# Hybrid decoder layer: turning q for two attention units at once, and moving the tokens' scales of the first part into the second

## The chip, the core and the metric

The kernel is written for one Trainium2 core and runs on one. Five engines work from their own queues, in the order of each queue, and wait for each other by semaphores: TensorE (PE, matmuls and transposes), VectorE (DVE), ScalarE (ACT), GpSimd (POOL) and SyncE (SP, which here only issues DMAs). The metric is the device time of one execution in microseconds (us); less is better.

## What is computed

One layer of a decoder with attention and a short convolution side by side, in float32: 512 tokens, width 2048.

```python
h = rms_norm(x, norm_gain)
q, k, v, g_attn, c_b, c_c, c_h, g_conv = split(h @ w_in)
q, k = partial_rope(rms_norm(q, q_gain)), partial_rope(rms_norm(k, k_gain))   # 16 and 4 heads of 64
y_attn = sliding_window_attention(q, k, v, sinks) * silu(g_attn)              # window 128
y_conv = c_b * conv3(c_c * c_h) * silu(g_conv)
x = x + concat(y_attn, y_conv) @ w_out
gate = sigmoid(rms_norm(x, gate_gain) @ w_ple_gate + b_ple_gate)
x = x + gate * rms_norm(p @ w_ple_proj, ple_gain)
```

The attention's probabilities are `exp(s - m) / (sum + exp(sink - m))` with `s` the scaled scores inside the window.

## The kernel before

Every float32 product is made of three: operands are split into a rounded high half and a low rest (`halves`: an ACT cast, then a DVE subtraction), and PE multiplies high by high, low by high and high by low. The large matmuls save products by a fast scheme of blocks (`run_step`, line 241), which needs sums of weight blocks (L189) and their halves (L199, L200) in time for each step. One step is 12 matmuls of 128x512.

The program has three parts. The **first** makes k and v (L515) and then q in 28 steps (L241). `kv` are four tiles of 128x512 in the pool `rowp`, one for each block of 128 tokens; q is left in four quarters `qs[t, n]`, `t` a half of the tokens and `n` a half of the heads. x enters unnormalised, so the tokens' scale `r_x = rsqrt(mean x^2)` is applied later: `tok["x"]` is that scale and `rx2_tok` its square. For the norm of q's heads `square_q` sums squares into `rq[t, n]` (called `msq`), and `rstd_q` makes of it the factor: DVE multiplies by `rx2_tok` (L566) and scales (L301), POOL takes the power -1/2 (L306), and DVE multiplies by `r_x` (L570). `rx2_rows` turns `rx2_tok` into rows: DVE spreads it into `rb` (L650), PE transposes four blocks (L653), and ACT copies the bank into `rx2` (L742), which `zc` (L892) needs.

The **second** part is the attention, in 16 units: `order` runs over the kv heads `j` = 2, 3, 0, 1 and inside over the four blocks `n` of 128 tokens. Unit `u` has four heads. Around the units run seven products `gemm_tile` (L719, 48 matmuls each) for the convolution's first columns, and four blocks of the embedding product (`e_block`, L878). PE's order is the order of the code. `at(when, fn)` puts work at a tick; one tick comes every six matmuls of `gemm_tile`. For a unit at tick `when`: `turn_q` at `when - 3`, `scores` at `when`, `turn` (transposes of the probabilities, L827, split into `pth` and `ptl`) at `when + 5`, `values` (L837, L838, then copied to `up` and added into DRAM by two DMAs from POOL's queue) at `when + 7`.

`turn_q` transposes two blocks of q into one half of `psm` (L786), a PSUM bank that stays one tile with two halves, used in turn. ACT then copies 64 partitions, rounded, into one half of `st` (L790), and DVE subtracts to get the rest into the other half (L791), and so again for the other 64 partitions. `scores` multiplies by k's halves `khh` and `kll` (L799, L800); DVE adds the mask and takes the maximum (L805), and ACT's four exponentials (L812) and that of the sink (L817) follow. `make_k` uses the same `psm`, two blocks at a time (L749, copied to `kr` by L750).

In the second part only PE's order is that of the code: a scheduler orders ACT, DVE, POOL and SP from the dependences and its own costs, and the order in which the code issues work only weighs in. In the first part and the third the code orders all engines.

The **third** part holds eight more groups of 28 steps, with the output product and the gate.

Of the kernel before, what the change touches and what calls it, by code (L numbers as in the profile page):

```python
# [30 lines left out]
def f32(ap):  # L31
    return ap.bitcast(F32)
# [3 lines left out]
def hymba_layer(ctx: ExitStack, tc: tile.TileContext, io):  # L36
# [14 lines left out]
    nc = tc.nc  # L51
# [8 lines left out]
    rowp = ctx.enter_context(tc.tile_pool(name="rowp", bufs=4, side="right", reuse_waits="tile"))  # L60
# [18 lines left out]
    def itile(name):  # L79
        return pools["io"].tile([P, T], F32, tag="io", name=name)  # L80
# [38 lines left out]
    def soon(table, s, fn, *args):  # L119
        table.setdefault(s, []).append((fn, args))  # L120
# [406 lines left out]
    tok = {}  # L527
# [41 lines left out]
    def times_token(ms, r):  # L569
        tt(ms, ms, r.unsqueeze(2).broadcast_to(ms.shape), op=ALU.mult)  # L570
# [18 lines left out]
    def rstd_q(t, n):  # L589
        blocks = slice(2 * t, 2 * t + 2)  # L590
        head_rstd(rq[t, n], rx2_tok[:, blocks])
        times_token(rq[t, n], tok["x"][:, blocks])

    def rope_q(t, n):
        rope(q_of(t, n), 0, slice(2 * t, 2 * t + 2), mtile)
# [45 lines left out]
    for t in range(2):  # L641
        for b in range(2):
            soon(after, 21 + t + b, square_q, t, 1, b, itile)
        soon(after, 24 + t, rstd_q, t, 1)
    rows_ps = []

    def rx2_rows():

        rb = itile("rb").rearrange("p (b t) -> p b t", t=P)
        nc.vector.tensor_copy(rb, rx2_tok.unsqueeze(2).broadcast_to([P, NB, P]))  # L650
        rows_ps.append(ps_t.tile([P, T], F32, name="pst"))
        for b in range(NB):
            nc.tensor.transpose(rows_ps[0][:, b * P : (b + 1) * P], rb[:, b, :], ident)  # L653

    soon(after, 25, rx2_rows)
    ptile = []

    def load_p():
# [18 lines left out]
    kk = second.enter_context(tc.tile_pool(name="kk", bufs=8, reuse_waits="tile"))  # L677
    vvp = second.enter_context(tc.tile_pool(name="vvp", bufs=1, reuse_waits="tile"))
    ap = second.enter_context(tc.tile_pool(name="ap", bufs=2, reuse_waits="tile"))
    misc = second.enter_context(tc.tile_pool(name="misc", bufs=9, side="right", reuse_waits="tile"))  # L680
    pe = second.enter_context(tc.tile_pool(name="pe", bufs=1, side="right", reuse_waits="tile"))
    cw = second.enter_context(tc.tile_pool(name="cw", bufs=2, side="right", reuse_waits="tile"))
    ps_s = second.enter_context(tc.tile_pool(name="ps_s", bufs=2, space=PSUM, reuse_waits="tile"))
    ps_g = second.enter_context(tc.tile_pool(name="ps_g", bufs=2, space=PSUM, reuse_waits="tile"))
    ps_o = second.enter_context(tc.tile_pool(name="ps_o", bufs=1, space=PSUM, side="right", reuse_waits="tile"))
    ps_m = second.enter_context(tc.tile_pool(name="ps_m", bufs=1, space=PSUM, side="right", reuse_waits="tile"))

    psm = ps_m.tile([P, 2, 2 * P], F32, name="psm")

    def mtile(name):  # L690
        return misc.tile([P, T], F32, tag="m", name=name)
# [5 lines left out]
    def at(when, fn):  # L697
        later.append((when, len(later), fn))
# [31 lines left out]

    for t in range(2):
        rope_q(t, 1)
        for b in range(2):
            at(19 + 2 * t + b, lambda t=t, b=b: square_q(t, 0, b, mtile))
        at(21 + 2 * t, lambda t=t: rstd_q(t, 0))
        at(24 + 2 * t, lambda t=t: rope_q(t, 0))
    mask = cw.tile([P, 2 * P], F32, name="mask", bufs=1)
    nc.gpsimd.dma_start(mask, io["mask"])
    vv = vvp.tile([P, NB, NKV, 2, HD], F32R, name="vv")
    khh, kll = [None] * NKV, [None] * NKV  # L740
    rx2 = mtile("rx2")
    nc.scalar.copy(rx2, rows_ps[0])  # L742

    def make_k(t):
        kr = mtile("kr")
        for i in range(2):
            pb = psm[:, i]
            for b in range(2):
                nc.tensor.transpose(pb[:, b * P : (b + 1) * P], kv[2 * i + b][:, t * P : (t + 1) * P], ident)  # L749
            nc.scalar.activation(kr[:, i * 2 * P : (i + 1) * 2 * P], pb, AF.Copy, scale=kq_g)  # L750
        for hf in range(2):
            j = 2 * t + hf
            own, oth = slice(hf * HD, hf * HD + HD), slice((1 - hf) * HD, (1 - hf) * HD + HD)
            khh[j], kll[j] = (kk.tile([P, T], F32R, tag="k", name=n) for n in ("khh", "kll"))
            nc.scalar.copy(khh[j][own], kr[own])
            nc.scalar.copy(khh[j][oth], kr[own])
            tt(kll[j][own], kr[own], f32(khh[j][own]), op=ALU.subtract)
            tt(kll[j][oth], kr[own], f32(khh[j][own]), op=ALU.subtract)

    def make_v():  # L760
        for b in range(NB):
# [2 lines left out]
            nc.scalar.activation(hi, src, AF.Copy, scale=r)  # L764
            stt(vv[:, b, :, 1], src, r, f32(hi), op0=ALU.mult, op1=ALU.subtract)

    at(4, lambda: make_k(1))
    at(6, make_v)
    at(7, lambda: make_k(0))


    rs = const.tile([P, NB, NH], F32, name="rs")
    turns_done = [0]

    def attention(j, n, when):

        lo = 0 if n else P
        cell = {}

        def turn_q():  # L780
            turns_done[0] += 1
            pt = psm[:, turns_done[0] % 2].rearrange("p (f t) -> p f t", t=P)
            q = qs[n // 2, j // 2][:, n % 2]
            for f in range(2):
                s = j % 2 * 2 * P + f * P
                nc.tensor.transpose(pt[:, f], q[:, s : s + P], ident)  # L786
            st = cell["q"] = cw.tile([P, 2, 2, P], F32R, name="st")
            for hf in range(2):
                own, oth = slice(hf * HD, hf * HD + HD), slice((1 - hf) * HD, (1 - hf) * HD + HD)
                nc.scalar.copy(st[own, :, hf], pt[own])  # L790
                tt(st[oth, :, hf], pt[own], f32(st[own, :, hf]), op=ALU.subtract)  # L791

        def scores():
            sc = [ps_s.tile([P, 2, 2 * P], F32, name="pss") for _ in range(2)]
            ks = slice(n * P + lo - P, (n + 1) * P)
            for r in range(4):
                q = cell["q"][:, r // 2, r % 2]
                out = sc[r // 2][:, r % 2, lo:]
                nc.tensor.matmul(out, q, khh[j][:, ks], start=True, stop=False)  # L799
# [17 lines left out]
            nc.scalar.activation(sk, sk, AF.Exp)  # L817
            tt(sums, sums, sk, op=ALU.add)
            nc.vector.reciprocal(rs[:, n, 4 * j : 4 * j + 4], sums)
            cell["t"] = t  # L820
# [21 lines left out]
            nc.gpsimd.dma_start(rows, up[:HD])  # L842
            cell["add"] = lambda: nc.gpsimd.dma_start(rows, up[HD:], accum_op=ALU.add)

        at(when - 3, turn_q)
        at(when, scores)
        at(when + 5, turn)
        at(when + 7, values)
# [635 lines left out]
```

## Time and profile before

| what | value |
|---|---|
| median of 3 runs | 947.1 us (946.58 to 948.57) |
| the profiled execution | 947.2 us, its span 945.4 us |
| mean granted clock of TensorE | 0.99 |
| first part's steps (L241) stop for the transposes of `rb` | 120.9 us |
| first product of the second part (L719) | 138.5 us |
| first scores (L799) | 181.5 us |
| last product of the attention's values (L838) | 301.6 us |

A row of the timeline gives start, duration, engine, line, operation, output and inputs with their shapes, and in brackets how long the engine sat idle before it and who ended that. A row of waits gives who waited for whom, then microseconds in total, times, and the longest. Matmuls overlap, so PE's durations add up to more than the distance of their starts; in an undisturbed stretch starts are 0.227 us apart.

### The profile page before, as it was taken

What the parts mean: (1) busy time and instruction counts of PE and PEld (TensorE: products, weight loads), DVE (VectorE), ACT (ScalarE), POOL (GpSimd) and SP (SyncE); (2) the same over time, 40 slices, a digit from 0 to 9 for tenths busy, and PEclk for the clock granted to TensorE, in tenths of its full rate; (3) what the DMA queues carried; (4) which work ended last, traced back from release to release, by engine and by line L of the source; (5) the groups of instructions that cost most, each with busy time, mean ns of one, the idle gap of its engine ahead of it and who ended that gap; (6) DMA issues with size and microseconds to landing.
All of it is one profiled execution on the core that took longest, in us unless ns stands there. A gap on an engine that the chain in (4) does not pass through costs nothing.

```text
span 945.4 us, 12136 instructions
## 1 busy us (share of the span) xinstructions
PE 914.5 (97%) x4208; PEld 757.5 (80%) x4208; DVE 728.4 (77%) x1091; ACT 548.2 (58%) x897; POOL 152.2 (16%) x200
## 2 busy tenths in 40 slices
PE   9999969988899999999999999999999999999997
PEld 7888847867787888888888888888888888888886
DVE  6877966677675767677767778989767786999778
ACT  7767726577685344445444436865566676674453
POOL 4231121242222000100110020010220112001100
PEclk9999979999999999999999999999999999999999
DMA  8999424624446886634834888795997996578747
GB/s 303 367 281 322 157 85 158 230 73 84 90 84 145 298 275 196 163 107 146 254 92 130 235 245 236 253 237 128 276 348 205 218 285 166 133 226 268 186 134 212
DMA packets 69086, 189.84 MB, mean 201 GB/s; under 512 B 8096, under 2 KB 14560, under 8 KB 69024
## 3 DMA queue, kind: packets, MB, share of 16 engines
q1 hardware_dynamic: 47520, 131.09, 40.5%
q0 software_dynamic: 21360, 57.96, 27.5%
q8 instruction: 33, 0.54, 0.2%
q14 instruction: 29, 0.24, 0.1%
q10 hardware_dynamic: 144, 0.01, 0.0%
HBM read 159.67 MB, written 29.36 MB: 200 GB/s over the span
## 4 chain that ended last, share of the span: by engine, by line
PE 82%; DVE 7%; ACT 6%; issue 2%; POOL 1%; DMA 1%; SPq 0%; DVEq 0%; ACTq 0%; POOLq 0%
PE psp L241 64%; PE psp L515 4%; PE psg L719 4%; PE pst L241 3%; ACT prob L812 3%; PE pst L997 2%; PE pss L878 1%; DVE wl L200 1%; PE pst L1361 1%; PE pst L878 1%; POOL msq L306 1%; DVE ptl L200 1%; DVE prob L805 1%; DVE st L791 1%; DMA x<-in_x 1%
## 5 line engine op out<-in xcount | busy, mean ns | idle before, releaser
L241 PE MATMUL psp<-wh,form 128*128 128x512 f32 x1280 | 395.4, 390 | 0.0
L241 PEld LDWEIGHTS psp<-wh,form 128*128 128x128 f32 x1280 | 239.3, 188 | 49.1
L241 PE MATMUL psp<-wl,form 128*128 128x512 f32 x640 | 249.3, 390 | 0.0
L200 DVE TENSOR_TENSOR wl<-wy,wh 128x1024 fp32r<-128x1024 f32 x108 | 131.8, 1222 | 55.5 <-ACT wh L199 54.6
L199 ACT CAST wh<-wy 128x1024 fp32r<-128x1024 f32 x108 | 113.5, 1051 | 93.4 <-PE psp L241 71.1
L241 PEld LDWEIGHTS psp<-wl,form 128*128 128x128 f32 x640 | 120.1, 188 | 25.5 <-DVE wl L200 0.4
L200 DVE TENSOR_TENSOR wl<-wx,wh 128x1024 fp32r<-128x1024 f32 x72 | 88.0, 1223 | 50.8 <-ACT wh L199 50.8
L241 PE MATMUL psp<-wh,hsh 128*128 128x512 f32 x304 | 119.6, 393 | 0.0
L199 ACT CAST wh<-ws 128x1024 fp32r<-128x1024 f32 x72 | 75.9, 1054 | 75.1 <-PE psp L241 54.4
L241 PE MATMUL psp<-wh,hsl 128*128 128x512 f32 x304 | 119.0, 392 | 0.0
L241 PE MATMUL psp<-wl,hsh 128*128 128x512 f32 x304 | 119.0, 392 | 0.0
L199 ACT CAST wh<-wx 128x1024 fp32r<-128x1024 f32 x72 | 75.6, 1052 | 72.4 <-PE psp L241 51.3
L200 DVE TENSOR_TENSOR wl<-ws,wh 128x1024 fp32r<-128x1024 f32 x72 | 88.1, 1223 | 28.9 <-ACT wh L199 28.7
L189 DVE TENSOR_TENSOR wy<-wy,ws 128x1024 f32<-128x1024 f32 x72 | 87.7, 1218 | 0.0
L241 PEld LDWEIGHTS psp<-wl,hsh 128*128 128x128 f32 x304 | 57.5, 189 | 12.2
L241 PEld LDWEIGHTS psp<-wh,hsh 128*128 128x128 f32 x304 | 57.7, 190 | 11.8
L241 PEld LDWEIGHTS psp<-wh,hsl 128*128 128x128 f32 x304 | 57.5, 189 | 11.9
L719 PE MATMUL psg<-hsh,wh 128*128 128x512 f32 x112 | 46.5, 415 | 0.0
L169 POOL DMA_DIRECT2D wy<-in_w_mid x16 | 14.0, 874 | 201.5 <-DVE wy L189 108.7
L719 PE MATMUL psg<-hsh,wl 128*128 128x512 f32 x112 | 44.8, 400 | 0.0
L719 PE MATMUL psg<-hsl,wh 128*128 128x512 f32 x112 | 44.6, 399 | 0.0
L199 ACT CAST wh<-raw 128x1024 fp32r<-128x1024 f32 (+1 forms) x29 | 29.2, 1008 | 21.9 <-PE psp L241 15.6
(221 smaller groups left out, 1339.3 us busy)
## 6 DMA issues: line engine op xcount, KB each, us to landing
ws<-in_w_mid SPq DMA_DIRECT2D x40, 512.0 KB, 4.6
wx<-in_w_mid SPq DMA_DIRECT2D x24, 512.0 KB, 3.9
wy<-in_w_mid SPq DMA_DIRECT2D x20, 512.0 KB, 7.5
h<-form POOLq DMA_DIRECT2D x32, 256.0 KB, 5.7
wy<-in_w_mid POOLq DMA_DIRECT2D x16, 512.0 KB, 8.9
raw<-in_w_in SPq DMA_DIRECT2D x16, 512.0 KB, 4.0
wx<-in_w_out SPq DMA_DIRECT2D x16, 512.0 KB, 6.6
ws<-in_w_out SPq DMA_DIRECT2D x16, 512.0 KB, 5.7
```

Of the source, the lines that this page charges most:

```text
L169: nc.gpsimd.dma_start(t, w[n, r, j, c], accum_op=ALU.add)
L189: tt(y, y, got[g, "s1" if f == 6 else "s0", c], op=ALU.add)
L199: nc.scalar.copy(h, src)
L200: tt(l, src, f32(h), op=ALU.subtract)
L241: nc.tensor.matmul(ps[t][:, cols], a, w[:, i, cols], start=start and first and i == 0 and n == 0, stop=last and i == 1 and n == 2, skip_gr ...
L306: nc.gpsimd.tensor_tensor(out, ms, e, op=ALU.pow)
L515: nc.tensor.matmul(kv_ps[t // 2][:, t % 2], hs[k][a][:, t * P : (t + 1) * P], kv_split[c][w][:, i], start=k == 0 and n == 0, stop=k == KT ...
L719: nc.tensor.matmul(ps, w[:, k % 8], a, start=k == 0 and n == 0, stop=k == KT - 1 and n == 2)
L791: tt(st[oth, :, hf], pt[own], f32(st[own, :, hf]), op=ALU.subtract)
L812: nc.scalar.activation(t[:, r, lo:], t[:, r, lo:], AF.Exp, scale=r_q[:, r : r + 1], bias=negm[:, r : r + 1], accum_out=sums[:, r : r + 1],)
L878: nc.tensor.matmul(banks[t], a, w[:, k], start=k == 0 and i == 0, stop=k == 1 and i == 2)
L997: nc.tensor.transpose(pt[:, b], quads[b // 2][:, b % 2, f * P : (f + 1) * P], ident)
```

## The change

Four things. (a) `rstd_q` no longer multiplies by `r_x`; `token_q` does, and is called in the second part at ticks 8 and 9 for the heads needed first and at 27 and 28 for the others. (b) `rx2_rows` moves into the second part: `rb` is made at its beginning and PE's four transposes come at tick 2. (c) `make_k` turns four blocks into a whole bank and evicts it with one ACT instruction. (d) `turn_q` turns two units at once (four transposes into a whole bank), four ticks ahead of the first of them; the rounded and the rest land in two tiles of 128x512, one for each pair of partitions' halves, in `rowp`, whose four buffers hold `kv` before. The pool `misc` gets two more buffers.

```diff
     def rstd_q(t, n):
         blocks = slice(2 * t, 2 * t + 2)
         head_rstd(rq[t, n], rx2_tok[:, blocks])
-        times_token(rq[t, n], tok["x"][:, blocks])
+
+    def token_q(t, n):
+        times_token(rq[t, n], tok["x"][:, 2 * t : 2 * t + 2])
...
-    rows_ps = []
-
-    def rx2_rows():
-
-        rb = itile("rb").rearrange("p (b t) -> p b t", t=P)
-        nc.vector.tensor_copy(rb, rx2_tok.unsqueeze(2).broadcast_to([P, NB, P]))
-        rows_ps.append(ps_t.tile([P, T], F32, name="pst"))
-        for b in range(NB):
-            nc.tensor.transpose(rows_ps[0][:, b * P : (b + 1) * P], rb[:, b, :], ident)
-
-    soon(after, 25, rx2_rows)
...
-    misc = second.enter_context(tc.tile_pool(name="misc", bufs=9, side="right", reuse_waits="tile"))
+    misc = second.enter_context(tc.tile_pool(name="misc", bufs=11, side="right", reuse_waits="tile"))
...
-    psm = ps_m.tile([P, 2, 2 * P], F32, name="psm")
...
     for t in range(2):
         rope_q(t, 1)
+        at(8 + t, lambda t=t: token_q(t, 1))
...
+        at(27 + t, lambda t=t: token_q(t, 0))
...
-    nc.scalar.copy(rx2, rows_ps[0])
+    rb = mtile("rb").rearrange("p (b t) -> p b t", t=P)
+    nc.vector.tensor_copy(rb, rx2_tok.unsqueeze(2).broadcast_to([P, NB, P]))
+
+    def rx2_rows():
+
+        pb = ps_t.tile([P, T], F32, name="pst")
+        for b in range(NB):
+            nc.tensor.transpose(pb[:, b * P : (b + 1) * P], rb[:, b, :], ident)
+        nc.scalar.copy(rx2, pb)
...
     def make_k(t):
         kr = mtile("kr")
-        for i in range(2):
-            pb = psm[:, i]
-            for b in range(2):
-                nc.tensor.transpose(pb[:, b * P : (b + 1) * P], kv[2 * i + b][:, t * P : (t + 1) * P], ident)
-            nc.scalar.activation(kr[:, i * 2 * P : (i + 1) * 2 * P], pb, AF.Copy, scale=kq_g)
+        pb = ps_m.tile([P, T], F32, name="psm")
+        for b in range(NB):
+            nc.tensor.transpose(pb[:, b * P : (b + 1) * P], kv[b][:, t * P : (t + 1) * P], ident)
+        nc.scalar.activation(kr, pb, AF.Copy, scale=kq_g)
...
+    at(2, rx2_rows)
     at(4, lambda: make_k(1))
...
+    def turn_q(j, t):
+
+
+        pt = ps_m.tile([P, T], F32, name="psm")
+        for b in range(2):
+            for f in range(2):
+                s = j % 2 * 2 * P + f * P
+                i = 2 * b + f
+                nc.tensor.transpose(pt[:, i * P : (i + 1) * P], qs[t, j // 2][:, b, s : s + P], ident)
+        for hf in range(2):
+            st = rowp.tile([P, T], F32R, tag="rows", name="st")
+            own, oth = slice(hf * HD, hf * HD + HD), slice((1 - hf) * HD, (1 - hf) * HD + HD)
+            nc.scalar.copy(st[own], pt[own])
+            tt(st[oth], pt[own], f32(st[own]), op=ALU.subtract)
+            turned[j, t, hf] = st
...
-        def turn_q():
-            turns_done[0] += 1
-            pt = psm[:, turns_done[0] % 2].rearrange("p (f t) -> p f t", t=P)
-            q = qs[n // 2, j // 2][:, n % 2]
-            for f in range(2):
-                s = j % 2 * 2 * P + f * P
-                nc.tensor.transpose(pt[:, f], q[:, s : s + P], ident)
-            st = cell["q"] = cw.tile([P, 2, 2, P], F32R, name="st")
...
             for r in range(4):
-                q = cell["q"][:, r // 2, r % 2]
+                i = 2 * (n % 2) + r // 2
+                q = turned[j, n // 2, r % 2][:, i * P : (i + 1) * P]
...
-        at(when - 3, turn_q)
+        if n % 2 == 0:
+            at(when - 4, lambda: turn_q(j, n // 2))
```

What the scheduler makes of it is seen in the engines' queues. The first place is DVE at the seam between the first part and the second. Before, these were its rows there (`wl_1288` is the low half of the weights of the first part's last step, `msq_1207` and `msq_1235` are q's `rq` for the heads needed first):

```order
L301 TENSOR_SCALAR msq_1207<-msq_1207 128x16
L570 TENSOR_TENSOR msk_717<-msk_717,r_x_1204 128x16
L765 SCALAR_TENSOR_TENSOR vv_1425<-kv_715,r_x_1204,vv_1425 128x4x64
L570 TENSOR_TENSOR msq_1207<-msq_1207,r_x_1204 128x16
L200 TENSOR_TENSOR wl_1288<-wy_581,wh_1287 128x1024
L566 TENSOR_TENSOR msq_1235<-msq_1235,rx2_tok_718 128x16
L576 TENSOR_TENSOR kv_713<-kv_713,msk_717 128x256
L301 TENSOR_SCALAR msq_1235<-msq_1235 128x16
L576 TENSOR_TENSOR kv_714<-kv_714,msk_717 128x256
L570 TENSOR_TENSOR msq_1235<-msq_1235,r_x_1204 128x16
L650 COPY rb_1307<-rx2_tok_718 128x512
L324 TENSOR_TENSOR z_788<-z_788,psp_1079 128x1024
```

Now the same stretch, and then the place further down where `rb` and the two products have gone:

```order
L301 TENSOR_SCALAR msq_1207<-msq_1207 128x16
L200 TENSOR_TENSOR wl_1287<-wy_581,wh_1286 128x1024
L566 TENSOR_TENSOR msq_1235<-msq_1235,rx2_tok_718 128x16
L570 TENSOR_TENSOR msk_717<-msk_717,r_x_1204 128x16
L764 SCALAR_TENSOR_TENSOR vv_1415<-kv_715,r_x_1204,vv_1415 128x4x64
L301 TENSOR_SCALAR msq_1235<-msq_1235 128x16
L324 TENSOR_TENSOR z_788<-z_788,psp_1079 128x1024
L200 TENSOR_TENSOR wl_1319<-raw_1259,wh_1318 128x1024
L576 TENSOR_TENSOR kv_713<-kv_713,msk_717 128x256
```

```order
L408 TENSOR_TENSOR rope_1408<-z_891,turn0_225 128x256
L734 COPY rb_1417<-rx2_tok_718 128x512
L409 TENSOR_TENSOR z_891<-rope_1408 128x16x8
L410 TENSOR_TENSOR z_891<-rope_1408 128x16x8
L200 TENSOR_TENSOR wl_1426<-raw_1282,wh_1425 128x1024
L200 TENSOR_TENSOR wl_1483<-raw_1284,wh_1482 128x1024
L764 SCALAR_TENSOR_TENSOR vv_1415<-kv_716,r_x_1204,vv_1415 128x4x64
L570 TENSOR_TENSOR msq_1207<-msq_1207,r_x_1204 128x16
L570 TENSOR_TENSOR msq_1235<-msq_1235,r_x_1204 128x16
L200 TENSOR_TENSOR wl_1537<-raw_1423,wh_1536 128x1024
```

The last split of the first part and the first one of the second part have moved ahead of the products with k; `rb` stands behind the turning of k and q, and the products with `msq` behind the splits of the jobs after it.

The second place is DVE in the attention, about where the second unit's `ptl` is made (`msq_1977` before and `msq_1981` now are `rq[0, 0]`). Before:

```order
L791 TENSOR_TENSOR st_1951<-psm_1383,st_1951 64x2x128
L816 TENSOR_TENSOR sk_1934<-attn_sinks_209,negm_1932 128x4
L562 TENSOR_REDUCE msq_1977<-sqq_1994 128x8
L566 TENSOR_TENSOR msq_1977<-msq_1977,rx2_tok_718 128x16
L301 TENSOR_SCALAR msq_1977<-msq_1977 128x16
L570 TENSOR_TENSOR msq_1977<-msq_1977,r_x_1204 128x16
L818 TENSOR_TENSOR sums_1933<-sums_1933,sk_1934 128x4
L819 RECIPROCAL rs_1428<-sums_1933 128x4
L791 TENSOR_TENSOR st_1983<-psm_1383,st_1983 64x2x128
L200 TENSOR_TENSOR ptl_2009<-pst_2003,pth_2008 128x512
L791 TENSOR_TENSOR st_1983<-psm_1383,st_1983 64x2x128
```

Now:

```order
L810 ISA negm_2029 128x1
L823 TENSOR_TENSOR sums_1933<-sums_1933,sk_1934 128x4
L301 TENSOR_SCALAR msq_1981<-msq_1981 128x16
L814 TENSOR_TENSOR negm_2029<-negm_2029,msq_1235 128x4
L824 RECIPROCAL rs_1419<-sums_1933 128x4
L787 TENSOR_TENSOR st_1972<-psm_1964,st_1972 64x512
L815 SCALAR_TENSOR_TENSOR negm_2029<-negm_2029,nsink_221 128x4
L570 TENSOR_TENSOR msq_1981<-msq_1981,r_x_1204 128x16
L821 TENSOR_TENSOR sk_2031<-attn_sinks_209,negm_2029 128x4
L200 TENSOR_TENSOR ptl_2006<-pst_2000,pth_2005 128x512
L200 TENSOR_TENSOR ptl_2015<-pst_2009,pth_2014 128x512
```

L301, whose result goes to POOL, and L570, which needs it back, are now five rows apart, and L301 has moved behind the scores of the next unit. On POOL the power of the other `rq` (`msq_2065` before, `msq_2061` now) stood between the two DMAs of the second unit, and now stands behind both:

```order
L306 TENSOR_TENSOR msq_1977<-msq_1977,half_neg_172 128x16
L842 DMA a2_85<-up_2000 64x4x128
L843 DMA a2_85<-up_2000 64x4x128
L842 DMA a2_85<-up_2083 64x4x128
L306 TENSOR_TENSOR msq_2065<-msq_2065,half_neg_172 128x16
L843 DMA a2_85<-up_2083 64x4x128
```

```order
L306 TENSOR_TENSOR msq_1981<-msq_1981,half_neg_172 128x16
L847 DMA a2_85<-up_1997 64x4x128
L848 DMA a2_85<-up_1997 64x4x128
L847 DMA a2_85<-up_2079 64x4x128
L848 DMA a2_85<-up_2079 64x4x128
L306 TENSOR_TENSOR msq_2061<-msq_2061,half_neg_172 128x16
```

The power has moved behind L848, which adds into what the DMA ahead of it writes.

The third place is ACT. Before, `st_1951` and `st_1983` were the turns of two units, and their copies stood on both sides of other work:

```order
L790 CAST st_1951<-psm_1383 64x2x128
L199 CAST pth_1967<-pst_1962 128x512
L790 CAST st_1951<-psm_1383 64x2x128
L812 ACTIVATE prob_1931,sums_1933<-prob_1931,negm_1932,msq_1235 128x256 x4
L817 ACTIVATE sk_1934<-sk_1934 128x4
L790 CAST st_1983<-psm_1383 64x2x128
L840 COPY up_2000<-pso_1997 128x512
L199 CAST pth_2008<-pst_2003 128x512
L790 CAST st_1983<-psm_1383 64x2x128
```

Now `st_1969` and `st_1972` are the two tiles of one turn for two units:

```order
L199 CAST pth_1960<-pst_1955 128x512
L786 CAST st_1969<-psm_1964 64x512
L199 CAST wh_2173<-raw_1909 128x1024
L817 ACTIVATE prob_1931,sums_1933<-prob_1931,negm_1932,msq_1235 128x256 x4
L822 ACTIVATE sk_1934<-sk_1934 128x4
L786 CAST st_1972<-psm_1964 64x512
L845 COPY up_1997<-pso_1994 128x512
```

Between its two copies stand a cast of weights and the exponentials of the third unit; so it is, with other units' exponentials, in six of the eight turns.

More of the change, by code (lines that the diff above doesn't have):

```diff
@@ L772, in hymba_layer @@
     rs = const.tile([P, NB, NH], F32, name="rs")
-    turns_done = [0]
+    def turn_q(j, t):
[11 more added lines that the diff above has]
+            turned[j, t, hf] = st
+    turned = {}
     def attention(j, n, when):
@@ L778, in attention @@
         cell = {}
-        def turn_q():
-            turns_done[0] += 1
-            pt = psm[:, turns_done[0] % 2].rearrange("p (f t) -> p f t", t=P)
-            q = qs[n // 2, j // 2][:, n % 2]
-            for f in range(2):
-                s = j % 2 * 2 * P + f * P
-                nc.tensor.transpose(pt[:, f], q[:, s : s + P], ident)
-            st = cell["q"] = cw.tile([P, 2, 2, P], F32R, name="st")
[L788 to L791, printed above, removed]
         def scores():
```

## The prediction, made before the changed kernel was run

> **What bounds the kernel now.** I read the page's busy shares first, then who TensorE (PE) waited for between 100 and 302 us, then busy time by stage.
>
> ```profile
> span 945.4 us, 12136 instructions
> ...
> PE 914.5 (97%) x4208; PEld 757.5 (80%) x4208; DVE 728.4 (77%) x1091; ACT 548.2 (58%) x897; POOL 152.2 (16%) x200
> ```
>
> ```profile
> PE psm L786 <- DVE st L791: 9.3, 4, 3.7
> PE pst L653 <- DVE rb L650: 9.2, 1, 9.2
> PE psm L749 <- ACT kr L750: 1.7, 2, 1.1
> PE pso L838 <- DVE ptl L200: 1.5, 2, 1.3
> PE pss L799 <- DVE st L791: 1.2, 1, 1.2
> ```
>
> ```profile
> 121.00:145.40 24.40, 14.12 (x56) 11.38 (x56) 13.91 (x44) 5.88 (x7) 7.03 (x5) 0.79 0.35 113
> 145.40:181.50 36.10, 35.48 (x160) 29.09 (x161) 24.49 (x35) 23.96 (x52) 8.13 (x15) 1.00 0.59 202
> 181.50:301.80 120.30, 108.07 (x584) 89.96 (x583) 87.26 (x308) 85.65 (x235) 35.13 (x38) 0.97 0.43 94
> 320.00:600.00 280.00, 280.00 (x1261) 232.25 (x1260) 210.81 (x207) 133.70 (x146) 20.71 (x28) 1.00 0.67 199
> ```
>
> The columns of the last answer are the stretch's length, busy time of PE, its weight loads, DVE, ACT and POOL, then granted clock and DMA. PE sets the end: 280.00 busy of 280 behind the attention. Nearly all its waiting lies where this change works: 9.2 us on one row at the seam of the two parts, 1.7 in `make_k`, and 9.3 + 1.2 + 1.5 = 12.0 in the attention. Each wait also costs clock:
>
> ```profile
> 131.00:135.00 4.00, 4.00 (x12) 3.20 (x11) 4.00 (x19) 0.00 (x0) 0.20 (x2) 0.50 0.47 128
> 197.00:200.00 3.00, 3.00 (x9) 2.43 (x10) 0.91 (x3) 2.31 (x10) 1.94 (x1) 0.53 0.01 3
> 232.00:235.00 3.00, 2.04 (x10) 1.74 (x11) 2.88 (x11) 1.44 (x4) 1.03 (x1) 1.00 0.16 23
> 250.40:254.00 3.60, 3.51 (x13) 2.88 (x14) 0.88 (x3) 0.90 (x3) 1.07 (x2) 0.59 0.71 201
> ```
>
> Behind the waits of 9.2, 3.14 and 3.66 us the granted clock is 0.50, 0.53 and 0.59; within 232 to 235, where PE waited about 1 us, it stays 1.00. In the attention that is 3.0 x 0.47 + 3.6 x 0.41 = 2.9 us more.
>
> **Part one, the seam.** These are PE's rows there, and what DVE, which it waits for, did:
>
> ```profile
> 120.71 0.39 PE L241 MATMUL psp<-wl,hsh 128*128 128x512 f32 x1
> 130.32 1.12 PE L653 MATMUL pst<-ident,rb 128*128 128x128 f32 x4 [9.22 <-DVE rb L650]
> ...
> 145.53 0.48 PE L878 MATMUL pss<-wh,ptsh 128*128 128x512 f32 x1
> ```
>
> ```profile
> 121.46 0.17 DVE L570 TENSOR_TENSOR msk<-msk,r_x 128x16 f32<-128x16 f32 x1
> ...
> 124.81 0.18 DVE L570 TENSOR_TENSOR msq<-msq,r_x 128x16 f32<-128x16 f32 x1 [2.79 <-POOL msq L306]
> 124.91 1.22 DVE L200 TENSOR_TENSOR wl<-wy,wh 128x1024 fp32r<-128x1024 f32 x1
> ...
> 129.75 0.17 DVE L570 TENSOR_TENSOR msq<-msq,r_x 128x16 f32<-128x16 f32 x1 [2.79 <-POOL msq L306]
> 129.84 0.42 DVE L650 COPY rb<-rx_tok 128x512 f32<-128x512 f32 x1
> 130.18 1.21 DVE L324 TENSOR_TENSOR z<-z,psp 128x1024 f32<-128x1024 f32 x1
> 131.31 1.22 DVE L200 TENSOR_TENSOR wl<-raw,wh 128x1024 fp32r<-128x1024 f32 x1
> 132.44 0.49 DVE L408 TENSOR_TENSOR rope<-kv,turn 128x64 f32<-128x64 f32 x3
> ...
> 136.79 1.23 DVE L200 TENSOR_TENSOR wl<-raw,wh 128x1024 fp32r<-128x1024 f32 x1
> ```
>
> DVE stands twice for POOL's power, with the last split of weights and `rb` behind it, and PE stands for `rb`. In the new order the two products of q's rows and `rb` leave this place. From 121.46 DVE then needs 1.14 for the split (ends 122.6), 0.7 for four short rows, 1.13 for `z`, 1.13 for job 0 (ends 125.6), 0.75 for the two products of k, the 4.35 us that lie between 132.44 and 136.79, and 0.42 for `rb`: 131.1.
>
> PE runs on at 120.94. Its two steps of 12 matmuls, 2.72 us each at the 0.227 us between rows of this stretch, end at 126.4; the split of 122.6 is in time for the second step, and job 0 for the first half tile. After 12 more matmuls, at 129.1, it needs `rb` and waits 2.0 us. Four transposes (0.45), 12 matmuls and `make_k`'s four transposes bring the first matmul of `e_block` to 134.85 instead of 145.53: **10.7 us**. Job 1 is split by 132.6 and is needed at 134.8. A wait of 2.0 us lies between the 1.4 that kept the clock and the 3.14 that lost it; I take it as kept, 1 us of clock is the other end. The second `make_k` loses its wait of 0.6: **11.3 us** in all. The new ACT copy of `rb`'s bank replaces the old one, 0.6 us, beside matmuls; without that cover it would hold only the first `zc`, 48 matmuls later.
>
> **Part two, the attention.** The new copies and subtractions are twice as wide. The trace has the width only from SBUF, in `make_k`:
>
> ```profile
> L790 ACT CAST st<-psm x32: 350/367/371, 166.4 to 284.8; 64x256 fp32r<-64x256 f32 x32
> L791 DVE TENSOR_TENSOR st<-psm,st x32: 417/422/428, 166.8 to 285.6; 64x256 fp32r<-64x256 f32 x32
> ...
> L755 ACT CAST khh<-kr x4: 616/620/621, 146.3 to 158.5; 64x512 fp32r<-64x512 f32 x4
> ...
> L757 DVE TENSOR_TENSOR kll<-kr,khh x4: 683/686/690, 147.0 to 159.2; 64x512 fp32r<-64x512 f32 x4
> ```
>
> Sixteen of each at 0.62 and 0.69 replace 32 at 0.37 and 0.42: ACT 9.9 for 11.7 us, DVE 11.0 for 13.5. Were they no cheaper by width (0.73, 0.84), nothing would be saved. These engines are busy 87 and 86 of 120 us, so the 2 us matter less than where the rows stand. Transposes stay 32 in number.
>
> ```profile
> 186.55 0.16 DVE L818 TENSOR_TENSOR sums<-sums,sk 128x4 f32<-128x4 f32 x1 [1.99 <-ACT sk L817]
> ...
> 189.37 0.69 DVE L898 TENSOR_TENSOR u<-psg,zc 128x512 f32<-128x512 f32 x1
> ...
> 197.80 0.17 DVE L301 TENSOR_SCALAR msq<-msq 128x16 f32<-128x16 f32 x1
> 201.00 0.17 DVE L570 TENSOR_TENSOR msq<-msq,r_x 128x16 f32<-128x16 f32 x1 [3.03 <-POOL msq L306]
> ```
>
> ```profile
> 196.82 0.69 PE L786 MATMUL psm<-ident,z 128*128 128x128 f32 x2 [3.14 <-DVE st L791]
> ...
> 204.91 0.39 PE L837 MATMUL pso<-pth,vv 128*128 128x512 f32 x1
> ...
> 250.49 0.44 PE L786 MATMUL psm<-ident,z 128*128 128x128 f32 x2 [3.66 <-DVE st L791]
> ```
>
> A turn now waits for the reads of the turn four or five ticks ago, not two or three, so the 9.3 us go, and the 1.2. What is late next? On the old clock: one subtraction of the second turn now lies inside the wait of 1.99, so `u` starts at about 189.1. `ptl` of the first unit then ends at 195.4, and PE is there at 194.9: 0.5 us. The rows from `u` to L301 took 8.43 us; two subtractions leave (0.9), one wide one (0.7), a weight split (1.2), four rows of scores (1.4) and small ones (0.2) come in: L301 at 200.1. L570 came 3.20 us behind L301, and the new order has only four rows between them: it **still stalls DVE** for 2 us, until 203.3. Both `ptl` of the second unit now stand behind it, and the first ends at 204.0. PE, relieved of 3.14 and of 1.4 us of clock, reaches that product at 200.5 instead of 204.91. It waits 3.5 us and loses the clock again, 1.4. POOL's second power now stands behind one more DMA, which adds into DRAM and itself waits for a DMA,
>
> ```profile
> POOL a L843 <- DMA a<-up: 33.5, 13, 4.3
> ```
>
> 2.6 us on average. DVE reaches that L301 only at about 211.6, when the DMA is done, so I price it at nothing; at most 4.3 us otherwise. Later turns find their reads done, as far as I followed the rows; for two later products and the scores behind them I leave 1.0 us. So 12.0 + 2.9 = 14.9 us of loss becomes 0.5 + 3.5 + 1.4 + 1.0 = 6.4: 8.5 us, and about 1.0 for seven interruptions fewer of PE's stream: **9.5 us**. The two ends: nothing, if DVE's other waits grow into the place, and 14.9 + 1.0 with no wait left.
>
> Behind the attention the order is the same, and loads stand at the same distance from its last matmul; no gain, no loss.
>
> **Two rules of the skill.** The Trainium skill, "TensorE: Matmul & The Clock Gate", section "Part 1: The HAM clock gate", halves the clock after an idle window of about 3.4 us. The trace agrees on the half (0.50) but lost it at 3.14 us; by the page my wait of 3.5 stands on the edge, and kept clock would make 1.4 us less. The Trainium skill, "PSUM — Partial Sum Buffer", section "PSUM bank collisions raise a hardware error", bars two engines from one bank on the same partitions. That speaks against a whole bank for one turn, since PE's next one waits for all four reads; but the old halves were no two buffers either, as L749's 1.7 us on `kr` show. Had they been independent, part one would bring 9.6.
>
> **The rivals.** (1) *Only the seam pays.* DVE's order in the attention is crowded (87 us of work, waits of 13 on ACT's exponentials, as the 1.99 above), so PE's waits return on `ptl` and scores: 947.2 - 11.3 = 935.9. For it: the one chain I followed gave back most. Against: 33 us in which DVE is idle. (2) *The powers' wait spares PE*, as it did before: 926.4 - 4.9 = 921.5. (3) *The seam's wait only moves.* `rb` now stands behind all turning of k and q; were that stretch to start no earlier than 132.44, `rb` would end at 137.2, six later than I have it, and with (1) the time is 942. (4) *Slower*: on ACT the second half's copy stands behind four exponentials in six of eight turns. If the scores find it late, each such turn costs up to 3.14 + 1.4 as at 196.82: six make 27 and the time 953. It decides from 20.8 / 6 = 3.5 us a turn; the chain above has the copy 1 us early.
>
> **The numbers.** The profiled execution took 947.2 us (span 945.4), the median of three is 947.1, so one sum serves both: 947.2 - 11.3 - 9.5 = **926.4**. Chances: forecast (922 to 930) 0.52, (1) 0.20, (2) 0.17, (3) 0.04, within 0.2% (about what a measurement tells from no change) 0.03, (4) 0.04. The range 918 to 938 takes in forecast, (2) and most of (1). Faster 0.93, same 0.03, slower 0.04.
>
> **What would show it.** The row of 9.22 us is gone, and the four transposes of `rb` wait about 2 us, 8 us after the place where PE stopped before. `e_block` begins near 135, and the clock before it stays 1.00. No wait of PE on L787 over 1 us. L570 of the attention still waits on POOL, and PE waits some 3.5 us for `ptl` of the second unit, near 190 on the new clock. I am wrong if `rb` ends behind 133, if PE waits for scores on `st`, or if the stretch from first scores to last product stays near 120 us.

## The result, and the profile after

The changed kernel takes **923.5 us** (median of 4 runs, 923.19 to 924.21) where the kernel before takes 947.1 (946.58 to 948.57): a ratio of 0.9749, with a 95% interval of 0.9732 to 0.9766. The profiled execution took 924.21 us, 22.99 less than the profiled one of before.

The page of the changed kernel, its span and busy shares:

```profile
span 922.4 us, 12085 instructions
...
PE 908.7 (99%) x4208; PEld 754.6 (82%) x4208; DVE 724.7 (79%) x1075; ACT 544.5 (59%) x879; POOL 151.4 (16%) x200
```

PE has the same 4208 matmuls, but its busy time fell from 914.5 to 908.7 us; its mean granted clock is 0.998, where it was 0.990. Its waits between 100 and 302 us (total, times, longest) were 23 us before. They are now:

```profile
PE pso L843 <- DVE ptl L200: 3.7, 2, 2.7
PE pst L740 <- DVE rb L734: 1.8, 1, 1.8
PE psp L241 <- DMA form<-h: 0.6, 1, 0.6
PE pso L842 <- ACT pth L199: 0.3, 1, 0.3
```

The rows of 9.3 on the subtraction of `st`, 9.2 on `rb`, 1.7 on `kr` and 1.2 under the scores are gone. What is left is 1.8 on `rb`, 3.7 on `ptl`, and a wait of 0.6 on a DMA that is new. By stage (the columns are length, busy time of PE, its weight loads, DVE, ACT and POOL, then granted clock and DMA):

```profile
121.00:134.50 13.50, 11.73 (x54) 9.40 (x53) 13.44 (x43) 4.69 (x6) 6.74 (x2) 1.00 0.38 119
134.50:170.00 35.50, 35.50 (x164) 29.40 (x163) 24.70 (x33) 24.49 (x50) 8.16 (x15) 1.00 0.70 240
170.00:277.80 107.80, 103.81 (x583) 88.03 (x582) 83.84 (x294) 83.03 (x221) 33.71 (x37) 1.00 0.45 100
277.80:877.00 599.20, 598.46 (x2709) 495.99 (x2708) 468.72 (x522) 325.09 (x437) 66.18 (x81) 1.00 0.73 212
```

The stretch at the seam is 13.50 long at a clock of 1.00, where it was 24.40 at 0.79. The attention, from the first scores to the first matmul behind its last product, is 107.80 long instead of 120.3. In both stretches DVE stood for POOL's power before the change. At the seam that wait is gone; in the attention it stays. PE at the seam (start, duration, and in brackets the idle time before the row):

```profile
131.26 0.66 PE L740 MATMUL pst<-ident,rb 128*128 128x128 f32 x4 [1.77 <-DVE rb L734]
...
134.88 0.48 PE L884 MATMUL pss<-wh,ptsh 128*128 128x512 f32 x1
```

DVE at the seam and in the attention, the rows of `rb`, of the four products of q's rows (L570) and of the two `ptl` of the second unit:

```profile
130.79 0.41 DVE L734 COPY rb<-rx_tok 128x512 f32<-128x512 f32 x1
...
134.19 0.25 DVE L570 TENSOR_TENSOR msq<-msq,r_x 128x16 f32<-128x16 f32 x2
...
191.52 0.17 DVE L570 TENSOR_TENSOR msq<-msq,r_x 128x16 f32<-128x16 f32 x1 [1.96 <-POOL msq L306]
...
191.80 1.29 DVE L200 TENSOR_TENSOR ptl<-pst,pth 128x512 fp32r<-128x512 f32 x2
...
202.70 0.18 DVE L570 TENSOR_TENSOR msq<-msq,r_x 128x16 f32<-128x16 f32 x1 [2.99 <-POOL msq L306]
```

At 134.19 two products run with no wait, where DVE stood 2.79 us for each before. At 191.52 DVE still stands 1.96 us, and the `ptl` that PE needs start right behind it. The wide copies and subtractions (minimum, median and maximum in ns):

```profile
L786 ACT CAST st<-psm x16: 566/582/587, 153.8 to 251.0; 64x512 fp32r<-64x512 f32 x16
L787 DVE TENSOR_TENSOR st<-psm,st x16: 683/690/694, 154.8 to 251.6; 64x512 fp32r<-64x512 f32 x16
```

### The profile page after: what moved, and what is told of

It reads as the page before. It is cut to its first block, busy times and chain, and to the rows that moved or that the text cites. A ratio compares the mean times of both kernels' runs of the same rounds, so it can differ in the third digit from the quotient of the medians.

```text
span 922.4 us, 12085 instructions
## 1 busy us (share of the span) xinstructions
PE 908.7 (99%) x4208; PEld 754.6 (82%) x4208; DVE 724.7 (79%) x1075; ACT 544.5 (59%) x879; POOL 151.4 (16%) x200
## 4 chain that ended last, share of the span: by engine, by line
PE 86%; DVE 6%; issue 3%; DMA 2%; ACT 1%; POOL 1%; SPq 0%; DVEq 0%; POOLq 0%; ACTq 0%
PE psp L241 64%; PE psg L708 6%; PE psp L515 5%; PE pst L241 4%; DMA a<-up 2%; PE pst L1003 2%; DVE wl L200 1%; PE pss L884 1%; PE pst L884 1%; PE pst L832 1%; DMA form<-h 1%; PE pss L804 1%; DVE z L1265 1%; PE pss L805 1%; PE pst L364 1%
## 5 line engine op out<-in xcount | busy, mean ns | idle before, releaser
L241 PE MATMUL pst<-wh,form 128*128 128x512 f32 (+1 forms) x132 | 39.6, 383 | 0.0
```

What stands on the lines that cost most here:

```text
L241: nc.tensor.matmul(ps[t][:, cols], a, w[:, i, cols], start=start and first and i == 0 and n == 0, stop=last and i == 1 and n == 2, skip_gr ...
```

## The experiments

Four marks of the trace serve to compare kernels: the first matmul of `e_block`, the first scores, the first matmul behind the attention's last product, and the end of the span. The table gives the lengths between them, in us of the profiled execution.

| kernel | to `e_block` | to scores | attention | rest | run's median |
|---|---|---|---|---|---|
| before | 145.53 | 36.00 | 120.26 | 643.6 | 947.1 |
| changed | 134.88 | 35.09 | 107.83 | 644.6 | 923.5 |
| e1, seam only | 135.89 | 35.99 | 121.41 | 643.6 | 939.2 |
| e2, turning only | 143.58 | 35.10 | 109.10 | 644.6 | 933.8 |
| e3, products back | 140.59 | 35.10 | 108.82 | 643.6 | 930.4 |
| e4, `rb` back | 134.54 | 35.07 | 108.77 | 643.7 | 924.2 |
| e5, products on POOL | 134.45 | 35.07 | 104.25 | 646.6 | 919.9 |
| e6, `rb` a tick later | 133.30 | 35.09 | 108.70 | 643.7 | 923.0 |
| e7, lead of two | 134.34 | 35.10 | 120.12 | 643.7 | 935.2 |
| e8, e5 and e6 | 133.27 | 35.08 | 104.29 | 643.7 | 918.5 |
| e9, lead of three | 134.69 | 35.10 | 111.91 | 644.0 | 927.4 |
| e10, changed, second profile | 134.74 | 35.10 | 108.74 | 644.3 | 924.7 (one run) |
| e11, changed, third profile | 133.92 | 35.11 | 107.75 | 643.7 | 922.3 (one run) |

The kernel before, measured again beside each set, had medians of 948.2 (e1 to e4), 948.8 (e5 to e8) and 948.0 (e9 to e11), so ratios are compared where 1 us matters.

### e1: the seam alone

```diff
 # against the kernel before
-        times_token(rq[t, n], tok["x"][:, blocks])
+    def token_q(t, n):
+        times_token(rq[t, n], tok["x"][:, 2 * t : 2 * t + 2])
...
+        at(8 + t, lambda t=t: token_q(t, 1))
-        at(21 + 2 * t, lambda t=t: rstd_q(t, 0))
+        at(21 + 2 * t, lambda t=t: (rstd_q(t, 0), token_q(t, 0)))
...
+    at(2, rx2_rows)
```

> The kernel before, with only the seam changed: `rb` is rounded and turned in the second part, and the products of q's first two rows are put off to ticks 8 and 9. Turning of k and q in halves of one bank, two rows of products and everything else in the attention are as before. My theory (two causes that add up: the seam 11.4 us, the turning 12.4 us): the wait on `rb` falls from 9.2 to about 1.8 us, the first matmul of e_block stands near 135.5, and the attention keeps its waits on the subtraction of `st` (9 to 10 us in sum): 936 us, between 934.5 and 937.5. Rival (the two parts lean on each other: the attention's waits shrink as soon as DVE enters it without the seam's delay): 931 us or less, and less than 6 us of waits on `st`. Rival (the seam's wait comes back on `st`): over 940.

Ratio 0.9909 (0.9892 to 0.9925), a gain of 8.6 us on 947.1. The median of 939.2 us lies outside the expected range, with 2 to 3 us less gain. The waits between 100 and 300 us:

```profile
PE psm L788 <- DVE st L793: 9.3, 4, 3.6
PE pst L741 <- DVE rb L735: 1.8, 1, 1.8
PE psm L750 <- ACT kr L751: 1.7, 2, 1.1
PE pso L840 <- DVE ptl L200: 1.3, 2, 1.1
PE pss L801 <- DVE st L793: 1.2, 1, 1.2
```

The wait on `rb` is the changed kernel's, and the four other rows of before are nearly untouched (only that on `ptl` is 1.3 instead of 1.5): the attention's waits do not shrink with the seam's. The expectation was off for two reasons that the table shows. It gave the seam the 1.7 us of `make_k`'s waits on `kr`, which belong to the whole bank (`e_block` at 135.89 instead of 134.88, and 0.9 us more up to the scores: 1.9 in sum). And this attention is 1.15 us longer than that of before with nearly the same waits, its clock 0.96 instead of 0.97. The clock differs behind two waits of 1.12 and 1.15 us that lie close together (in the kernel before 1.29 and 1.15); the first row is e1's, the second that of before:

```profile
206.00:209.50 3.50, 3.50 (x20) 2.93 (x20) 2.85 (x7) 3.30 (x9) 0.66 (x1) 0.74 0.20 37
```

```profile
216.00:219.00 3.00, 3.00 (x23) 2.73 (x22) 2.58 (x7) 2.95 (x6) 0.67 (x1) 1.00 0.24 44
```

e10 and e11 below show that the same program can differ in this way from run to run.

### e2: the turning alone

```diff
 # against the kernel before: make_k, turn_q, scores and the 11 buffers of `misc` as in the change, and
-        at(when - 3, turn_q)
+        if n % 2 == 0:
+            at(when - 4, lambda: turn_q(j, n // 2))
```

> The kernel before, with only the turning changed: k's four blocks and two units of q are turned into a whole bank, rounded in two tiles of 512 columns from the freed row buffers, one tick earlier. `rb` and the products of q stand as before. My theory: the seam keeps its 9.2 us on `rb`, the waits on `st` go, one or two waits on `ptl` of 2 to 4 us stay beside POOL's power, and the stretch from first scores to last product is 108 us instead of 120: 935 us, between 933.5 and 937. Rival (the attention's gain needs the products of the second pair of rows put off behind the power, too): the stretch is 112 us or longer, and the time 939 or more.

Ratio 0.9851 (0.9837 to 0.9866), a gain of 14.1 us on 947.1; by its own profile, 13.0 of the span. In the table: 1.95 before `e_block`, 0.9 behind it from `make_k`, 11.2 in the attention, and 1.0 lost in the rest. The 1.95 are 1.06 of `make_k`'s first wait and 0.9 by which the wait on `rb` is shorter, since other rows of DVE's order moved, too:

```profile
129.33 1.11 PE L653 MATMUL pst<-ident,rb 128*128 128x128 f32 x4 [8.32 <-DVE rb L650]
```

The gains of e1 and e2 add up to 22.7 us, where the whole change has 23.8 by the same reckoning. The attention takes 109.1 us, not 112 or longer, though both pairs of products stand right behind the power here, so putting off the second pair is not what the attention needs. DVE stands there for 1.96 and 2.73 us:

```profile
200.21 0.17 DVE L570 TENSOR_TENSOR msq<-msq,r_x 128x16 f32<-128x16 f32 x1 [1.96 <-POOL msq L306]
...
212.29 0.17 DVE L570 TENSOR_TENSOR msq<-msq,r_x 128x16 f32<-128x16 f32 x1 [2.73 <-POOL msq L306]
```

The first is the changed kernel's 1.96 to the last digit: six ticks later in the code moved the product by nothing here, since in both kernels the same four rows stand between L301 and L570 in DVE's order.

### e3 and e4: the products back, or `rb` back

```diff
 # e3, against the changed kernel
+        times_token(rq[t, n], tok["x"][:, blocks])
...
-        at(8 + t, lambda t=t: token_q(t, 1))
-        at(27 + t, lambda t=t: token_q(t, 0))
```

> The changed kernel, with the products of q's rows back right behind POOL's power (`rb` stays moved). My theory (what delays PE at the seam is DVE standing for POOL's power, not the place of `rb`): DVE stands twice for about 2.8 us before the last split of weights and before job 0; PE waits about 2.4 us for the split and 3 for job 0, and the clock falls; e_block's first matmul is near 141.5: 930 us, between 927 and 934. Rival (moving `rb` is what pays): PE's waits stay under 2 us in sum ahead of `rb`, e_block starts by 136, and the time is within 1.5 us of the changed kernel's 923.5.

```diff
 # e4, against the changed kernel: rb and its transposes as before
+    soon(after, 25, rx2_rows)
...
-    at(2, rx2_rows)
```

> The changed kernel, with `rb` and its transposes back in the first part (the products stay put off). My theory (DVE's waits for POOL's power are the cause): `rb` is done near 123.1, about 2 us after PE needs it, PE waits 2 us there instead of 1.8 us later, and the time is that of the changed kernel: 923.7 us, between 922.5 and 925. Rival (the move of `rb` pays of itself, since its copy and transposes are covered in the second part): at least 3 us slower than the changed kernel.

e3 took 930.4 us (ratio 0.9819, 0.9804 to 0.9833), e4 924.2 (0.9750, 0.9735 to 0.9764, against the changed kernel's 0.9749). PE's waits of e3 at the seam:

```profile
126.26 0.50 PE L241 MATMUL psp<-wl,hsh 128*128 128x512 f32 x1 [1.97 <-DVE wl L200]
132.32 0.50 PE L706 MATMUL psg<-hsh,wl 128*128 128x512 f32 x1 [3.05 <-DVE wl L200]
136.98 0.66 PE L736 MATMUL pst<-ident,rb 128*128 128x128 f32 x4 [0.59 <-DVE rb L730]
```

With `rb` moved and the products not, DVE stands 2.83 and 2.79 us again, and PE stands for whatever split of weights comes next in DVE's order; `e_block` starts 5.7 us later. With `rb` back and the products put off, there is one wait, of the old place and the new size:

```profile
122.78 0.66 PE L655 MATMUL pst<-ident,rb 128*128 128x128 f32 x4 [1.83 <-DVE rb L652]
```

With e2, which has neither, the four cases are complete (all with the new turning). `e_block` starts at 143.58 with neither, at 140.59 with `rb` moved alone (e3), at 134.54 with the products put off alone (e4), and at 134.88 with both. So putting off the products brings the whole of the seam's gain, 9.0 us, without the move of `rb`. That move, the larger part of the diff there, brings 3.0 us while the products stand in DVE's way (e2's and e3's intervals do not overlap), and once they are put off it makes no difference that the intervals could tell.

### e5, e6 and e8: the rest that is left

```diff
 # e5, against the changed kernel
     def token_q(t, n):
-        times_token(rq[t, n], tok["x"][:, 2 * t : 2 * t + 2])
+        r = tok["x"][:, 2 * t : 2 * t + 2]
+        nc.gpsimd.tensor_tensor(rq[t, n], rq[t, n], r.unsqueeze(2).broadcast_to(rq[t, n].shape), op=ALU.mult)
 # e6
-    at(2, rx2_rows)
+    at(3, rx2_rows)
 # e8: both
```

> The changed kernel, with the products of q's rows by `r_x` done by POOL, right behind its own power, in place of DVE. My theory (what is left in the attention is DVE standing 2.0 and 3.0 us for POOL's power, with `ptl` behind it): DVE shows no wait on the power, PE's wait of 2.66 us on `ptl` of the second unit falls to about 0.7 and the one of 1.08 goes, and there is no clock to lose: 920.7 us, between 919.5 and 922. Rival (DVE is late by its own work, since it does 84 us of work in 108): the waits on `ptl` stay over 2 us in sum, and the time is within 1 us of the changed kernel's 923.5. Rival (POOL's added rows hold up the sums into DRAM that stand behind them): 925 or more.

> The changed kernel, with the transposes of `rb` put one tick (six matmuls, 1.37 us) later. My theory (the 1.8 us that PE waits there are only the rest of DVE's queue): the wait falls to about 0.4, e_block begins 1.4 us earlier, near 133.5, and the time is 922.1, between 921 and 923. Rival (the wait moves to the turning of k behind it): e_block begins within 0.4 us of 134.9, and the time is that of the changed kernel.

> The changed kernel with both: products of q's rows on POOL, and the transposes of `rb` one tick later. My theory (the two rests add up): 919.3 us, between 918 and 921. Rival (one of them takes back what the other gives): no faster than the better of the two alone.

e5 took 919.9 us (ratio 0.9697, 0.9680 to 0.9715). POOL's own rows, its power and then the product:

```profile
188.20 2.92 POOL L306 TENSOR_TENSOR msq<-msq,half_neg 128x16 f32<-128x16 f32 x1 [5.86 <-DVE negm L815]
191.20 0.21 POOL L595 TENSOR_TENSOR msq<-msq,r_x 128x16 f32<-128x16 f32 x1
```

The product costs 0.21 us in both rows of the attention. The two at the seam are 1.20 and 3.98 us long on POOL (its spans are rough), and no row of PE or DVE waits for them:

```profile
129.57 3.98 POOL L595 TENSOR_TENSOR msq<-msq,r_x 128x16 f32<-128x16 f32 x1
```

DVE waits for no power any more. PE's waits in the attention of e5:

```profile
PE pso L844 <- DVE ptl L200: 0.6, 1, 0.6
PE pso L843 <- ACT pth L199: 0.3, 1, 0.3
```

The 2.66 is 0.62 and the 1.08 is gone, as expected; the attention is 104.25. So DVE's standing for POOL is shown as the cause of most of what the change left: 3.6 us of the attention. In this profile, the slowest of the four runs of e5, 2 us of it are given back behind the attention, in a wait of 2.0 on the same DMA as the 0.6 above.

e6 took 923.0 us (0.9729, 0.9715 to 0.9744), at the upper end of its range. The wait on `rb` fell to 0.43 and `e_block` starts at 133.30, 1.58 earlier, but the times of the two kernels cannot be told apart: this profile lost clock in the attention (108.70).

e8 took **918.5 us** (918.14 to 918.73; 0.9678, 0.9665 to 0.9692). Its interval lies below the changed kernel's, so it beats both kernels. In its profile both parts are there (`e_block` at 133.27, an attention of 104.29); but its interval overlaps that of e5, so that the time is better than e5's alone is not shown. PE waits 1.3 us in all between 100 and 302.

### e7 and e9: the lead of the turn

```diff
 # against the changed kernel; e9 has when - 3
-            at(when - 4, lambda: turn_q(j, n // 2))
+            at(when - 2, lambda: turn_q(j, n // 2))
```

> The changed kernel, with each turn of q issued two ticks ahead of its scores in place of four. My theory (the whole bank removed the waits because its reads lie far back, and the lead of four ticks is what keeps the scores from standing for `st`): the scores wait for `st`, some 1 to 2 us at several of the eight turns, 5 to 10 us in sum with the clock: 930 us, between 926 and 936. Rival (the lead does not matter, the merging alone pays): less than 1 us of waits on `st`, and the time within 1.5 us of 923.5.

> The changed kernel, with each turn of q issued three ticks ahead of its scores, the lead of the kernel before, in place of four. My theory (with a lead of two the scores waited 2.0, 2.5, 1.6, 2.7, 1.8 and 0.5 us for `st` and lost clock behind most of them; one tick is six matmuls, 1.37 us, more): waits of 0.6, 1.1, 0.2, 1.4 and 0.4 are left, about 3.7 us in sum, and the clock stays: 927 us, between 924.5 and 930. Rival (the whole bank alone pays, the lead only has to be three): no wait of the scores over 0.5 us, and the time within 1 us of the changed kernel's 923.5. Rival (the lead of four is all that pays): over 8 us of waits on `st`, and 932 or more.

e7 took 935.2 us (0.9855, 0.9840 to 0.9870), slower than expected but within its range, with 11.0 us of waits on `st` instead of 5 to 10; e9 927.4 (0.9788, 0.9766 to 0.9811). The waits of e7 between 100 and 302 us, then its attention:

```profile
PE pss L804 <- DVE st L787: 11.0, 6, 2.7
PE pst L740 <- DVE rb L734: 1.8, 1, 1.8
```

```profile
169.40:289.60 120.20, 109.17 (x584) 93.12 (x584) 84.33 (x294) 83.64 (x221) 33.83 (x37) 0.94 0.42 92
```

With a lead of two, the scores stand six times for `st`, and the attention is as long as it was before the change. The mean clock falls to 0.94: behind three of the waits (2.48, 1.60 and 2.74) it is 0.65, 0.50 and 0.50, behind the others (2.00, 1.76 and 0.46) it stays 1.00. With three, the lead of before, the waits of e9 are:

```profile
PE pso L843 <- DVE ptl L200: 3.8, 4, 2.4
PE pss L804 <- DVE st L787: 2.0, 1, 2.0
```

The time is as expected, but not the places of the loss: one wait on `st` of 2.0 instead of five short ones, and four on `ptl`. So of the 12.4 us turning two units at once gives 8.4 at the old lead (120.26 to 111.91), and the earlier tick the other 3.2 to 4.1. What in the turning gives the 8.4 no run takes apart: fewer turns, the wider copies, the whole bank, and room in `rowp` for the `st` of four units where `cw` had two came together.

### e10 and e11: the changed kernel's clock

> The changed kernel once more, for a second profile. My theory (whether a wait of about 2.66 us loses the clock is decided by where it falls, not by its length: three other kernels lost it behind 2.65, 2.65 and 2.67, the changed kernel kept it): the wait of 2.66 on `ptl` is there again; the clock behind it is 1.00 again or 0.55 to 0.75, and in the latter case the stretch from first scores to the first matmul of the last product's successor is 108.8 instead of 107.8. Rival (the changed kernel is different in kind there): 1.00 and 107.8 in every execution. The time is 923.5 within 0.7 either way.

> The changed kernel a third time, for a third profile; as the second: the wait of 2.66 is there, the clock behind it 1.00 or 0.55 to 0.75, and the stretch 107.8 or 108.8 with it.

924.66 and 922.30 us, a wider spread than I expected. The wait is in both (2.66 and 2.67). The 3.5 us from 192.5 on, in e10, e11 and the first profile (the wait ends at 192.41, 191.59 and 192.55; in e11 the clock is 1.00 from 191.59 on, too):

```profile
192.50:196.00 3.50, 3.50 (x19) 3.13 (x20) 2.42 (x10) 2.31 (x5) 1.74 (x2) 0.71 0.31 45
```

```profile
192.50:196.00 3.50, 3.50 (x26) 3.15 (x25) 3.08 (x11) 1.56 (x3) 1.74 (x2) 1.00 0.38 42
```

```profile
192.50:196.00 3.50, 3.45 (x23) 2.95 (x24) 3.05 (x11) 2.35 (x5) 1.74 (x2) 1.00 0.27 43
```

The same program with the same wait lost the clock once (0.71) and kept it twice. Where it is lost, the attention takes 108.74 instead of 107.8. That is 1.0 us and not the 1.7 of the slower clock (3.5 x 0.29 + 3.0 x 0.23 in the next stretch), as PE then comes later to the fourth unit's `ptl` and waits 0.38 there instead of 1.08.

## Why the prediction was right

The forecast was 926.4 us, and 923.5 was measured; on the profiled executions 20.8 us of gain stand against 22.99. The total is nearer than its largest term: the attention brought 2.9 more than forecast, and 1.0, put at nothing, was lost behind it. That the two partly cancel is luck. By its steps:

| step | predicted | measured |
|---|---|---|
| first matmul of `e_block` | 134.85 | 134.88 |
| wait on `rb` | 2.0, clock kept | 1.77, clock 1.00 |
| seam in all (to the first scores) | 11.3 | 11.56 |
| `ptl` of the first unit | 0.5 | none |
| `pth` of the second unit | none | 0.25 |
| DVE's first wait on the power | 2.0 | 1.96 |
| `ptl` of the second unit | 3.5 | 2.66 |
| clock behind it | 1.4 | 0 or 1.0 net |
| two later waits | 1.0 | 1.08, or 0.38 with the clock lost |
| attention in all | 9.5 | 12.4 |
| behind the attention | 0 | -1.0 |

**The seam** came out by its own chain. Two things in it were told apart only by the runs. The prediction let both the products and `rb` leave DVE's order there; e4 shows that the products alone do it, and e3 that `rb` alone does a third. And 1.9 us of the 11.56 are not the seam's but the turning's (e1), through `make_k`; the prediction had the first 1.0 of them inside its chain and the second as 0.6, where it is 0.9.

**The attention** brought 12.4 instead of 9.5: the mechanism was right and three terms were too large. The loss left was priced at 6.4 and was 0.25 + 2.66 + 1.08 = 4.0. Of that difference of 2.4, the clock is 1.4, the longer wait on `ptl` 0.8, and the first unit 0.25 (0.5 less the 0.25 on `pth`). The `ptl` of the second unit came when the chain said: PE goes on at 192.55, which is 204.1 on the old clock, 11.56 us later, and the forecast was 204.0. It was PE that came later, at 201.4 instead of 200.5. The remaining 0.5 of the 2.9 was not traced. The clock term was no error in kind: it was paid in one of three profiles of this kernel, and in e2, e3, e4 and e6 behind waits of 2.65 to 2.67. The Trainium skill, "TensorE: Matmul & The Clock Gate", section "Part 1: The HAM clock gate", calls the window of activity free-running and gives that as the reason why the ramp at a kernel's start varies from run to run. That a loss in the middle of a program varies in e10, e11 and the first profile would fit, but no run here shows the window itself. The same section of the Trainium skill has the clock halved after an idle window of about 3.4 us. Here pauses of 2.65 us were enough.

**Behind the attention** the step failed. "Loads stand at the same distance from its last matmul; no gain, no loss" is true of their order, not of their time. The 599.20 of the last stage is 598.20 before, for the same matmuls:

```profile
301.80:900.00 598.20, 598.08 (x2709) 496.00 (x2708) 468.65 (x522) 325.26 (x437) 65.92 (x81) 1.00 0.73 211
```

The chain of waits of the changed kernel from 277 to 302 us shows where it goes:

```profile
279.60 0.64 POOL a L848
280.24 9.70 DMA a<-up
...
290.24 3.44 DMA a<-up
...
293.69 0.03 SPq L158
...
294.71 5.56 DMA form<-h
300.27 0.14 issue
300.41 1.64 PE psp L241 x6
```

And SP's waits in the same stretch, and below them those of the kernel before from 301 to 325 us:

```profile
SPq L158 <- DMA a<-up: 16.4, 3, 8.3
```

```profile
SPq L158 <- DMA a<-up: 12.5, 2, 7.4
```

The load of `form` that PE needs at 300.41 is issued behind weight loads on SP (L158), and those wait, by the profile, for the last sums of the attention into DRAM (`a<-up`): 16.4 us here, 12.5 in the kernel before. Two things are later than before. POOL issues the first sum of the last unit 2.4 us behind the attention's end (280.24 against 277.80), as the sums ahead of it hold it up; before it was 1.1 us. In the three profiles whose attention takes 120 us or more that distance is 1.1 us, in the others 1.3 to 2.7. And from this first sum to the second it takes 10.0 us, before 5.0. So `form` is issued 16.9 us behind the attention's end instead of 13.0. The wait is not in every kernel with a shorter attention: it is 0.62 here, 0.2 in e10, 0.7 in e2 and 2.0 in e5, but none in e3, e4, e6, e8, e9 and e11, and e8's attention is as short as e5's. In the kernel before, PE waited for no `form`. What sets the DMA's own length from run to run stays open, and so do the other 0.4 of the 1.0.

**The rivals.** *Only the seam pays* falls with e2 and e1: the turning is the larger part. *The powers' wait spares PE* falls with the 2.66, and e5 prices it. *The seam's wait only moves* falls with `rb` at 130.79. *Slower* did not come, but its mechanism is real: at a lead of two (e7) the scores find `st` late at six places and the whole gain of the attention is lost. The lead of four had 1 us to spare by the prediction's chain, and no wait on `st` was seen.

## What to carry to other kernels

An engine that stands for a short result of another engine delays all that is queued behind it in its order; here two products of 0.17 us cost PE 9 us at the seam (e2 against e4). Put such an operation where its input is long done, or give it to the engine that makes the input, as e5 does. When PE waits for two engines to read a buffer in PSUM, turning twice as much at once can take the wait away, but only with a lead long enough for the whole chain of copies: each tick of six matmuls taken from the lead here cost 3 to 8 us. Then look at the next transfer behind the stage: here it took back 0.2 to 2.0 us in four of the profiles.

## What was not expected of the hardware

The clock: a wait of 2.66 us lost it in one of three executions of one program and kept it in two, so a single profile of this kernel is good to 1 us at best; four other kernels lost it behind 2.65 to 2.67, e9 behind 2.41, and e1 behind two waits of 1.12 and 1.15 us close together, which the kernel before survived:

```profile
198.80:202.30 3.50, 3.50 (x11) 2.77 (x12) 2.05 (x8) 2.65 (x11) 0.15 (x1) 0.52 0.40 37
237.00:240.50 3.50, 3.43 (x20) 2.99 (x21) 2.57 (x13) 0.97 (x3) 1.23 (x2) 1.00 0.37 116
```

These are the 3.5 us behind e9's waits of 2.41 (clock 0.52) and of 2.02 (1.00). POOL's power on 128x16 took 2.92 us at 188.20, its product of the same shape, right behind it, 0.21; two other rows of that product took 1.20 and 3.98, and why is open.
